# Two-layer transformer trunk: new order of the feed-forward units, later sums of one pair's rows, a second buffer for row sums

## The chip, the cores and the metric

One core of a Trainium2 chip. The metric is the device time of one execution in microseconds (us). Timed runs of the kernel before: 947.54, 944.46 and 944.89 us, median 944.89 us.

## The reference

Two decoder layers on 512 tokens of 1024 features, all in float32. Layer 0 mixes by causal pooling, layer 1 by differential attention; each mixer and each SwiGLU feed-forward is followed by a LayerNorm of the residual. The change touches the feed-forward and the LayerNorm ahead of it:

```
def _swiglu(x, w_gate, w_up, w_down):
    return (jax.nn.silu(x @ w_gate) * (x @ w_up)) @ w_down
...
for i in range(DEPTH):
    h = pool or attention
    x = _layernorm(ALPHA * x + h, ln_mix_g[i], ln_mix_b[i])
    x = _layernorm(ALPHA * x + _swiglu(x, w_gate[i], w_up[i], w_down[i]), ln_ffn_g[i], ln_ffn_b[i])
```

The hidden width is 2816, that is 22 blocks of 128 features.

## The kernel before

Float32 products are made of three products of split operands: a tile t is cast to a high part h (a cast on ACT, "CAST"), and DVE forms the low part l = t - h; PE then sums h·h, h·l and l·h. In the trace g_25h and g_25l are the two parts of weight chunk 25.

**Feed-forward, gate phase.** `hid` holds the 22 rows (blocks) of the hidden activation, transposed, in 22 rows of 512 tokens. The work is a list of units, in the order of the table `ORDER`. A plain unit f makes one hidden block: two products of 24 matmuls of width 512 (gate and up), then silu on ACT and a multiplication on DVE (`gated`, L737). A pair p(k) makes rows k and k+11 at once by a Winograd scheme of seven products in place of eight, each of 24 matmuls of width 256 (`strassen`; products in the order of `GATE`: P1, Q5, P6, Q3, P7, P2, Q4; accumulators A, B, C in PSUM). Of pairs 3 and 4 (`PRE`) the products P1 and P2 are made at the start of the phase, and their result waits in a tile `pre_g`; these are the begun pairs, of five products each (`BEGUN`: P6, Q5, P7, Q3, Q4). A pair needs four raw weight rows of 128x1024 from the wall of weights in HBM, three of its seven chunks are sums of rows (L696, DVE), every chunk is split (cast L699 on ACT, low part L702 on DVE). The products of a pair take as left operands blocks of x (`xt`) and four sums of blocks of x (`xs`), which `sums_of_x` computes step by step (L750 adds two blocks whole; L765, L767, L770, L774 the rest; casts L753, low parts L756) with four spare places in rows of `hid` as scratch (`spare`).

How far ahead chunks are made is a fixed number: after product j of a pair the steps up to chunk j + `lookahead` are issued; after a product of a plain unit, up to j + 5. Raw rows are fetched by SP into five buffers (L141), each as soon as a buffer is free; buffers of split weights are six pairs.

**Work on the side.** Generators that are stepped once after each product (`catch_up`):
- `weight_sums` / `sum_terms(k)`: sums of rows of the down-projection weights. POOL loads them (`load_terms`: two loads L804, then a third that adds in flight, L805, into rows 7 to 10 of `hid` or into the buffer of tag "gb", named b_3, b_5, ... in the trace); DVE adds twice (L810, L811); ACT stores to the DRAM tensor `tsum` (L815); then the next terms are loaded. Terms 0 and 1 are loaded at the start, 3 after unit f3 (it needs the gb buffer), each other one behind the store of the terms two before it.
- `sum_hidden(k)`: sums of the four quarters of the hidden rows k and k+11: four DVE operations of 128x256 (L836 to L839), a cast on ACT into the tile v (L841), the low part on DVE (L843), a store on ACT's queue into the DRAM tensor `ssum` (L845). v has one buffer. `SPARED` = {3: 7, 4: 10} delays pair 3's sums to product Q3 of pair 7 and pair 4's to product Q3 of pair 10.

**Down phase.** Another Winograd scheme over items d_0, d_1, ...: raw rows r_j from the wall or from `tsum`, cast to d_jh (L153, ACT), low part d_jl (L154, DVE); left operands from `hid` by a cast and a subtraction into xs, or from `ssum`; `prepare(j + 5, j + 4)` works five weight items ahead; products at L1066 into P and Q. d_5 is the last item of its first product P1, whose left operand comes from row 10 of `hid`, made by pair 10.

**LayerNorm and turning.** Four row blocks of x (128 tokens each) are normalized in turn and transposed by PE; ACT applies scale and bias into y (L280), ACT and DVE split y into `xt` (`turn`). `load_gb` loads scale and bias of the next LayerNorm into the gb buffer (L207, L208, on SP's queue); `affine` uses them on DVE (L258, L259).

Engines run their queues in program order; ACT's queue also issues the stores L815 and L845, SP's the raw rows, r rows and load_gb, POOL's the terms.

Of the kernel before, what the change touches and what calls it, by code (L numbers as in the profile page):

```python
# [18 lines left out]
P = 128  # L19
S = 512  # L20
# [28 lines left out]
SPLIT = (3, 4, 5, 6, 7, 8, 9, 10)  # L49
EARLY = (1, 0)  # L50
PRE = SPLIT[:2]
SUMS = 2
SPARED = {3: 7, 4: 10}


ORDER = "f0 f1 f2 f3 f4 p3 f5 p4 p5 p6 p7 p8 p9 p10".split()


def units(layer):
# [2 lines left out]


def lookahead(k, p):
    return 4 if k in PRE else 6 if k > 5 else 4 if p in ("P1", "Q5", "P6") else 5


AFFINE = {("P6", 2): (0, 1), ("P6", 3): (1, 1), ("Q3", 1): (2, 0), ("Q3", 2): (3, 0)}
# [6 lines left out]
def trunk(ctx, tc, x, wall, pscale, lam_p, subln, table, lng, lnb, band, first, onehot, out):  # L75
# [129 lines left out]
    def load_gb(n):  # L205
        gb = keep.tile([P, 2, D], F32, tag="gb", name=f"gb{n}")
        nc.sync.dma_start(out=gb[:, 0, :], in_=lng[n : n + 1, :].broadcast_to([P, D]))  # L207
        nc.sync.dma_start(out=gb[:, 1, :], in_=lnb[n : n + 1, :].broadcast_to([P, D]))  # L208
        gbs[n] = gb
# [107 lines left out]
        for i in (1, 0):  # L317
            nc.vector.tensor_tensor(ls[i], ys[i], hs[i].bitcast(F32), op=ALU.subtract)

    def turn(n, s):  # L320
        transposed(n, s)
        turned(n, s)

    flip, flipped = transposed, turned

# [239 lines left out]
    def ffn(layer, late):  # L565
# [7 lines left out]
        with tc.tile_pool(name=f"ffn{layer}", bufs=1) as fp:  # L573
# [168 lines left out]
            def spare(row):  # L742
                return hid[:, row : row + 2, :].rearrange("p r (a t) -> p (r a) t", a=2)

            def sums_of_x():

                r0, r1, r2, r3 = spare(3), spare(14), spare(5), spare(16)

                def whole(t, a, b):
                    tt(t, quarter(a, 0, b).bitcast(F32), quarter(a, 1, b).bitcast(F32), op=ALU.add)  # L750

                def high(m, t):
                    nc.scalar.copy(xs[:, m, 0], t)  # L753

                def low(m, t):
                    tt(xs[:, m, 1], t, xs[:, m, 0].bitcast(F32), op=ALU.subtract)  # L756

                whole(r2, 0, 0)
                yield
                whole(r3, 0, 1)  # L760
                yield
                whole(r0, 1, 0)
                whole(r1, 1, 1)
                yield
                tt(r1, r0, r1, op=ALU.subtract)  # L765
                high(0, r1)
                tt(r0, r2, r0, op=ALU.subtract)  # L767
                high(2, r0)
                yield
                tt(r2, r1, r2, op=ALU.subtract)  # L770
                high(1, r2)
                low(0, r1)
                yield
                tt(r3, r3, r2, op=ALU.add)  # L774
                high(3, r3)
                low(1, r2)
                yield
                low(2, r0)
                yield
                low(3, r3)  # L780
                yield
# [48 lines left out]
            def sum_hidden(k):  # L830

                first, second = hid[:, k, :256], hid[:, k, 256:]
                a12, a22 = hid[:, k + HALF, :256], hid[:, k + HALF, 256:]
                u = fp.tile([P, 2, 256], F32, tag="u", name=f"u{layer}_{k}", bufs=1)
                v = fp.tile([P, 2, 2, 256], F32R, tag="v", name=f"v{layer}_{k}", bufs=1)
                tt(u[:, 0, :], first, second, op=ALU.subtract)  # L836
                tt(second, second, a22, op=ALU.subtract)
                tt(u[:, 1, :], a12, first, op=ALU.subtract)
                tt(u[:, 1, :], u[:, 1, :], second, op=ALU.add)  # L839
                yield  # L840
                nc.scalar.copy(v[:, :, 0, :], u)  # L841
                yield
                tt(v[:, :, 1, :], u, v[:, :, 0, :].bitcast(F32), op=ALU.subtract)  # L843
                yield
                nc.scalar.dma_start(out=ssum[:, :, :, k, :], in_=v.bitcast(F32))  # L845
# [77 lines left out]
            by_half = [(0, 0, ks[0]), (1, 0, ks[0]), (0, 0, ks[1]), (1, 0, ks[1])]  # L923
            by_half += [(0, 1, ks[1]), (0, 1, ks[0])]
            halved = [(w, e, ks[b]) for b in range(2) for w, e in ((0, 0), (1, 0), (0, 1))]
            pre_g = {k: fp.tile([P, S], F32, name=f"g{layer}_{k}") for k in PRE}
            pre_a = {}
            products = [0]

            def turn_late():  # L930
                products[0] += 1
                if products[0] in late:
                    late[products[0]]()

            ready_first = 2 * early + 2 * len(PRE) + (early == 0)
            for lo in (0, 256):
# [34 lines left out]
            def plain(f):  # L971
                k = f // 2
                j = number[f, 0]
                a = (bank(f"g{layer}_{f}"), bank(f"u{layer}_{f}"))
                for i in range(2):
                    product(a[i], j + i, 0, S, by_part if f == i == 0 else None)
                    if f >= SUMS:
                        next(sums, None)
                    ahead(j + i + 5)
                    catch_up()  # L980
                gated(order[f], *a)
                if f < SB:
                    affine(n - 1, f, f // 2)
                if f % 2 or f == 0:
                    weight_sums()
                if f == 3:
                    load_terms(3)
                if f % 2 and k not in SPARED:
                    behind.append(sum_hidden(k))

            def strassen(k):
# [10 lines left out]
                for p in BEGUN if begun else GATE:  # L1002
# [30 lines left out]
                    elif p == "Q4":  # L1033
                        tt(first, both(g0), first, op=ALU.mult)
                        tt(second, both(g1), second, op=ALU.mult)
                if k < HALF - 1:
                    weight_sums()
                if k not in SPARED:
                    behind.append(sum_hidden(k))

            for kind, i in units(layer):
                (plain if kind == "f" else strassen)(i)
            load_gb(n - 1)
            while behind:
                catch_up()
            fetched[0] = divided[0] = c1 + FB
# [29 lines left out]
            for p in DOWN:  # L1076
# [7 lines left out]
                for i in range(together):  # L1084
                    j = j0 + i
                    prepare(j + 5, j + 4)
                    if p == "Q4":
                        if i == together - 1:
                            prepare(len(items), len(items))
                            ready(c1 + FB + 2)  # L1090
                        for s in range(2):
                            if i == s:
                                spread_of(n, s)
                            if i == s + 1:
                                norm(n, s)
                    if (p, i) == ("Q4", 2) and not final:
                        tall_step(2)
                    multiply(j, accs, range(2))
                    if (p, i) in AFFINE:
                        affine(n - 1, *AFFINE[p, i])  # L1100
                        if final and (p, i) == list(AFFINE)[-1]:
                            load_gb(n)
# [41 lines left out]
    def attention():  # L1144
        n = 2
        with tc.tile_pool(name="attn", bufs=1) as ap:
# [406 lines left out]
            for s in range(SB):  # L1553
                acc = gather(1, s, ws)
                if s == 0:
                    ready(where[0] + 1)
                for d in range(2):
                    residual(s, d, acc[d], 1.0)
                    stat(n, s, d)
                spread_of(n, s)  # L1560
                if s > 0:
                    turn(n, s - 1)
                norm(n, s)
                ready(where[0] + (min(s + 1, WBUFS - 4) if s < 3 else 4))
            base[0] = where[0]

    def later(n, s):
        return lambda: turn(n, s)

    ffn(0, {3: later(0, 2), 5: later(0, 3)})  # L1570
    attention()
    ffn(1, {2: later(2, 3)})


def buckets(rel):
# [105 lines left out]
```

## Time and profile before

| | |
|---|---|
| profiled execution | 949.09 us |
| its span | 947.3 us (1.8 us of the execution lie around it) |
| median of the timed runs | 944.89 us (944.46 to 947.54) |
| PE, DVE, ACT, POOL busy | 926.9, 803.5, 518.7, 127.3 us |
| HBM traffic | 217.39 MB, mean 229 GB/s |
| the first down product begins, layer 0 and layer 1 | about 265 us, about 829 us |

A row of a timeline gives start and duration of an instruction, its engine, line and tiles, and in brackets how long its engine stood idle before it and what ended that. Matmuls overlap: their starts are 0.227 us apart at width 512 and 0.120 us at width 256, while each is listed as 0.39 and 0.28 us long, so a stop of PE is read from starts, as the distance of two starts less that pitch.

### The profile page before, as it was taken

How to read it: one execution, taken by the hardware profiler on the slowest of the kernel's cores; microseconds unless marked ns; L12 is line 12 of the kernel's file. 1: busy time of each engine (PE TensorE's matmuls, PEld its weight loads, DVE VectorE, ACT ScalarE, POOL GpSimd, SP SyncE). 2: the span in 40 equal slices, each digit the busy share in tenths (PEclk: the TensorE clock that was granted, in tenths of full speed). 3: DMA queues.
4: the chain of work that ended last, by engine and by line, in shares of the span. 5: the costliest groups of instructions: out<-in, count | busy, mean ns of one | idle time of the engine just before them, and what ended most of it. 6: DMA issues, size and time to landing. Idle time of an engine off the chain costs nothing.

```text
span 947.3 us, 14914 instructions
## 1 busy us (share of the span) xinstructions
PE 926.9 (98%) x5662; PEld 824.0 (87%) x5662; DVE 803.5 (85%) x1190; ACT 518.7 (55%) x826; POOL 127.3 (13%) x152
## 2 busy tenths in 40 slices
PE   9999999999989999999999999999999999989996
PEld 8988999999978888888888888988999999968885
DVE  7988789999878897868888877868799999768888
ACT  6663335554545467767878754824444545554460
POOL 4111211110001201201112000210111110001101
PEclk9999999999999999999999999999999999999999
DMA  8496989986777988965666522693988985778962
GB/s 236 157 291 217 291 281 298 274 268 233 235 229 273 348 292 236 223 199 153 163 135 184 151 67 68 195 322 104 310 282 280 310 263 195 244 229 271 372 212 89
DMA packets 87765, 217.39 MB, mean 229 GB/s; under 512 B 15332, under 2 KB 26852, under 8 KB 87694
## 3 DMA queue, kind: packets, MB, share of 16 engines
q1 hardware_dynamic: 45148, 123.46, 38.1%
q0 software_dynamic: 18768, 58.20, 25.2%
q10 hardware_dynamic: 23778, 34.78, 10.1%
q8 instruction: 44, 0.72, 0.3%
q14 instruction: 27, 0.22, 0.1%
HBM read 179.70 MB, written 36.72 MB: 228 GB/s over the span
## 4 chain that ended last, share of the span: by engine, by line
PE 57%; DVE 23%; DMA 8%; issue 6%; ACT 4%; POOL 1%; ACTq 1%; DVEq 0%; POOLq 0%; SPq 0%
PE P L1066 10%; PE Q L1066 6%; PE A L906 6%; DVE raw L696 4%; PE C L906 3%; DMA raw<-in_wall 3%; DMA b<-in_wall 3%; PE va L1220 2%; PE B L906 2%; PE s L1289 2%; PE q L179 2%; PE q L181 2%; PE k L179 2%; PE k L181 2%; PE q L180 2%
## 5 line engine op out<-in xcount | busy, mean ns | idle before, releaser
L696 DVE TENSOR_TENSOR raw<-raw,raw 128x1024 f32<-128x1024 f32 x64 | 78.2, 1222 | 8.9 <-DMA raw<-in_wall 8.0
L153 ACT CAST xs<-hid 128x512 fp32r<-128x512 f32 (+1 forms) x60 | 34.7, 581 | 26.8 <-DVE hid L873 26.8
L154 DVE TENSOR_TENSOR xs<-hid,xs 128x512 fp32r<-128x512 f32 (+1 forms) x60 | 38.4, 642 | 7.8 <-ACT xs L153 7.8
L1309 ACT ACTIVATE p<-p,mn 128x128 f32<-128x128 f32 (+3 forms) x64 | 35.2, 552 | 14.1 <-DVE mn L1304 14.1
L841 ACT CAST v<-u 128x512 fp32r<-128x512 f32 x22 | 13.7, 621 | 52.3 <-DVE u L839 34.9
L280 ACT ACTIVATE y<-pt,bT,gT 128x128 f32<-128x128 f32 x72 | 27.1, 456 | 23.5 <-PE pt L266 18.0
L804 POOL DMA_DIRECT2D b<-in_wall x20 | 14.1, 708 | 189.3 <-DMA tsum<-b 58.3
L865 POOL DMA_DIRECT2D xs<-ssum x24 | 17.5, 727 | 148.9 <-PE Q L1066 73.0
L229 POOL TENSOR_TENSOR rs<-rs,mhalf 128x1 f32<-128x1 f32 x16 | 12.9, 806 | 138.3 <-DVE rs L228 93.6
L1304 DVE CUSTOM_DVE_ANT_0 p<-s,bias 128x128 f32<-128x128 f32 (+3 forms) x64 | 28.0, 485 | 1.1 <-PE s L1289 1.1
L1012 ACT COPY hid<-C 128x512 f32<-128x512 f32 x16 | 9.4, 588 | 35.1 <-PE A L906 12.2
L804 POOL DMA_DIRECT2D hid<-in_wall x24 | 20.9, 913 | 56.0 <-DMA tsum<-hid 28.8
L753 ACT CAST xs<-hid 128x1024 fp32r<-128x1024 f32 x8 | 8.4, 1050 | 28.5 <-DVE hid L765 15.6
L220 DVE BATCH_NORM_STATS2 st<-res 128x6 f32<-128x512 f32 x32 | 22.2, 695 | 1.1
L843 DVE TENSOR_TENSOR v<-u,v 128x512 fp32r<-128x512 f32 x22 | 15.1, 686 | 9.0 <-ACT v L841 9.0
L805 POOL DMA_DIRECT2D hid<-in_wall x12 | 14.8, 1233 | 55.2 <-DMA hid<-in_wall 55.2
L737 DVE TENSOR_TENSOR hid<-sg,u 128x512 f32<-128x512 f32 x12 | 8.2, 686 | 13.5 <-PE u L181 7.3
L154 DVE TENSOR_TENSOR xt<-y,xt 128x512 fp32r<-128x512 f32 x18 | 12.2, 689 | 8.7 <-ACT xt L153 8.7
L1323 DVE SCALAR_TENSOR_TENSOR p<-p,sm,p 128x128 f32<-128x128 f32 (+3 forms) x32 | 17.6, 551 | 1.1
L805 POOL DMA_DIRECT2D b<-in_wall x10 | 12.3, 1230 | 43.2 <-DMA b<-in_wall 43.2
L154 POOL TENSOR_TENSOR sql<-sq,sqh 128x512 fp32r<-128x512 f32 x7 | 9.3, 1324 | 60.5 <-ACT sqh L153 60.5
L259 DVE TENSOR_TENSOR res<-res,gb 128x512 f32<-128x512 f32 (+1 forms) x20 | 16.0, 799 | 0.7
(1206 smaller groups left out, 3583.3 us busy)
## 6 DMA issues: line engine op xcount, KB each, us to landing
raw<-in_wall SPq DMA_DIRECT2D x130, 512.0 KB, 5.7
r<-tsum SPq DMA_DIRECT2D x40, 512.0 KB, 4.3
hid<-in_wall POOLq DMA_DIRECT2D x36, 512.0 KB, 8.0
b<-in_wall POOLq DMA_DIRECT2D x30, 512.0 KB, 6.3
r<-in_wall SPq DMA_DIRECT2D x30, 512.0 KB, 5.6
tsum<-hid ACTq DMA_DIRECT2D x24, 512.0 KB, 5.8
ssum<-v ACTq DMA_DIRECT2D x22, 512.0 KB, 5.5
tsum<-b ACTq DMA_DIRECT2D x20, 512.0 KB, 5.7
```

The costliest lines, as they stand in the source:

```text
L153: nc.scalar.copy(dst_h, src)
L154: (low or nc.vector).tensor_tensor(dst_l, src, dst_h.bitcast(F32), op=ALU.subtract)
L179: nc.tensor.matmul(acc, ah, bh, start=start, stop=False)
L181: nc.tensor.matmul(acc, al, bh, start=False, stop=stop)
L280: nc.scalar.activation(y[:, k, :], pt[:, k * P : (k + 1) * P], AF.Identity, bias=bT[:, n, kk : kk + 1], scale=gT[:, n, kk : kk + 1],)
L696: tt(t, raws[pair[0]], raws[pair[1]], op=ALU.add)
L804: nc.gpsimd.dma_start(out=t[:, j], in_=src[:, j])
L805: nc.gpsimd.dma_start(out=t[:, 0], in_=src[:, :, 1], accum_op=ALU.add)
L906: nc.tensor.matmul(acc[:, f * 256 : (f + 1) * 256], w[:, c], x[:, kk, :], start=start and i == 0, stop=stop and i == len(todo) - 1, skip_g ...
L1066: nc.tensor.matmul(accs[s], x[:, k, r], y[:, c], start=first and k == 0 and e == 0, stop=last and k == m - 1 and e == 2, skip_group_check= ...
L1304: nc.vector.tensor_tensor_reduce(out=p, in0=accs[c], in1=biases[h][:, w - 1 :: -1] if w < S else biases[h][:, ::-1], op0=ALU.add, op1=ALU. ...
L1309: nc.scalar.activation(p, p, AF.Exp, bias=mn[:, q, c : c + 1], scale=-1.0, accum_out=sm[:, q, c : c + 1],)
```

## The change

1. `ORDER` becomes f0 f1 f2 f3 **p3 f4 p4 f5** p5 ...: a plain unit behind each begun pair (before: f3 f4 p3 f5 p4 p5). The rows of the wall follow. `lookahead` is 4 in begun pairs and 6 in all others.
2. `pre_g` of pairs 3 and 4 lies in rows 2 and 13 of `hid`, and v has two buffers.
3. `weight_sums` runs after f0 f1 f2 f4 p4 f5 p5 ... p9 (before: f0 f1 f3 p3 f5 p4 p5 ... p9): 11 times a layer as before.
4. `SPARED` = {2: 6}: the sums of hidden rows of pair 2 are made in pair 6; those of pairs 3 and 4 right behind their pairs.
5. Blocks 2 and 3 of x are turned with y written straight into the two scratch places of `sums_of_x` that held those blocks' whole sums, so two DVE additions (L750) a layer go; `sums_of_x` starts at f1 and is a step shorter. In layer 1 the turn of block 2 moves from the end of attention to the start of the feed-forward.
6. `load_gb` moves from the end of the gate phase to the second item of the down product Q5.

```diff
--- before.py
+++ after.py
@@ -49,11 +49,12 @@
 SPLIT = (3, 4, 5, 6, 7, 8, 9, 10)
 EARLY = (1, 0)
 PRE = SPLIT[:2]
-SUMS = 2
-SPARED = {3: 7, 4: 10}
-
-
-ORDER = "f0 f1 f2 f3 f4 p3 f5 p4 p5 p6 p7 p8 p9 p10".split()
+SUMS = 1
+NO_SUMS = (3, 3, 10)
+SPARED = {2: 6}
+
+
+ORDER = "f0 f1 f2 f3 p3 f4 p4 f5 p5 p6 p7 p8 p9 p10".split()
 
 
 def units(layer):
@@ -62,7 +63,7 @@
 
 
 def lookahead(k, p):
-    return 4 if k in PRE else 6 if k > 5 else 4 if p in ("P1", "Q5", "P6") else 5
+    return 4 if k in PRE else 6
 
 
 AFFINE = {("P6", 2): (0, 1), ("P6", 3): (1, 1), ("Q3", 1): (2, 0), ("Q3", 2): (3, 0)}
@@ -317,9 +318,9 @@
         for i in (1, 0):
             nc.vector.tensor_tensor(ls[i], ys[i], hs[i].bitcast(F32), op=ALU.subtract)
 
-    def turn(n, s):
+    def turn(n, s, kept=None):
         transposed(n, s)
-        turned(n, s)
+        turned(n, s, kept)
 
     flip, flipped = transposed, turned
 
@@ -742,9 +743,12 @@
             def spare(row):
                 return hid[:, row : row + 2, :].rearrange("p r (a t) -> p (r a) t", a=2)
 
+            second_half = spare(3), spare(14)
+
             def sums_of_x():
 
-                r0, r1, r2, r3 = spare(3), spare(14), spare(5), spare(16)
+                r0, r1 = second_half
+                r2, r3 = spare(5), spare(16)
 
                 def whole(t, a, b):
                     tt(t, quarter(a, 0, b).bitcast(F32), quarter(a, 1, b).bitcast(F32), op=ALU.add)
@@ -758,9 +762,6 @@
                 whole(r2, 0, 0)
                 yield
                 whole(r3, 0, 1)
-                yield
-                whole(r0, 1, 0)
-                whole(r1, 1, 1)
                 yield
                 tt(r1, r0, r1, op=ALU.subtract)
                 high(0, r1)
@@ -832,7 +833,7 @@
                 first, second = hid[:, k, :256], hid[:, k, 256:]
                 a12, a22 = hid[:, k + HALF, :256], hid[:, k + HALF, 256:]
                 u = fp.tile([P, 2, 256], F32, tag="u", name=f"u{layer}_{k}", bufs=1)
-                v = fp.tile([P, 2, 2, 256], F32R, tag="v", name=f"v{layer}_{k}", bufs=1)
+                v = fp.tile([P, 2, 2, 256], F32R, tag="v", name=f"v{layer}_{k}", bufs=2)
                 tt(u[:, 0, :], first, second, op=ALU.subtract)
                 tt(second, second, a22, op=ALU.subtract)
                 tt(u[:, 1, :], a12, first, op=ALU.subtract)
@@ -923,14 +924,16 @@
             by_half = [(0, 0, ks[0]), (1, 0, ks[0]), (0, 0, ks[1]), (1, 0, ks[1])]
             by_half += [(0, 1, ks[1]), (0, 1, ks[0])]
             halved = [(w, e, ks[b]) for b in range(2) for w, e in ((0, 0), (1, 0), (0, 1))]
-            pre_g = {k: fp.tile([P, S], F32, name=f"g{layer}_{k}") for k in PRE}
+            pre_g = {k: hid[:, r, :] for k, r in zip(PRE, (2, 2 + HALF))}
             pre_a = {}
             products = [0]
 
             def turn_late():
+                if products[0] in late:
+                    turn(n - 1, late[products[0]], second_half)
                 products[0] += 1
-                if products[0] in late:
-                    late[products[0]]()
+
+            turn_late()
 
             ready_first = 2 * early + 2 * len(PRE) + (early == 0)
             for lo in (0, 256):
@@ -981,7 +984,7 @@
                 gated(order[f], *a)
                 if f < SB:
                     affine(n - 1, f, f // 2)
-                if f % 2 or f == 0:
+                if f not in NO_SUMS:
                     weight_sums()
                 if f == 3:
                     load_terms(3)
@@ -1033,14 +1036,13 @@
                     elif p == "Q4":
                         tt(first, both(g0), first, op=ALU.mult)
                         tt(second, both(g1), second, op=ALU.mult)
-                if k < HALF - 1:
+                if k not in NO_SUMS[1:]:
                     weight_sums()
                 if k not in SPARED:
                     behind.append(sum_hidden(k))
 
             for kind, i in units(layer):
                 (plain if kind == "f" else strassen)(i)
-            load_gb(n - 1)
             while behind:
                 catch_up()
             fetched[0] = divided[0] = c1 + FB
@@ -1096,6 +1098,8 @@
                     if (p, i) == ("Q4", 2) and not final:
                         tall_step(2)
                     multiply(j, accs, range(2))
+                    if (p, i) == ("Q5", 1):
+                        load_gb(n - 1)
                     if (p, i) in AFFINE:
                         affine(n - 1, *AFFINE[p, i])
                         if final and (p, i) == list(AFFINE)[-1]:
@@ -1558,18 +1562,15 @@
                     residual(s, d, acc[d], 1.0)
                     stat(n, s, d)
                 spread_of(n, s)
-                if s > 0:
+                if 0 < s < 3:
                     turn(n, s - 1)
                 norm(n, s)
                 ready(where[0] + (min(s + 1, WBUFS - 4) if s < 3 else 4))
             base[0] = where[0]
 
-    def later(n, s):
-        return lambda: turn(n, s)
-
-    ffn(0, {3: later(0, 2), 5: later(0, 3)})
+    ffn(0, {3: 2, 5: 3})
     attention()
-    ffn(1, {2: later(2, 3)})
+    ffn(1, {0: 2, 2: 3})
 
 
 def buckets(rel):
```

The first place is ACT at the end of pair 10 and the start of the down phase of layer 0 (sg_10: the gates of pair 10; v_9, v_10, v_4: hidden sums of pairs 9, 10 and 4; xs: left operands of the down phase). Before:

```order
L841 CAST v_4_2935<-u_4_2934 128x2x256
L1032 ACTIVATE sg_10_0_2964<-B_4_683 128x512
L1026 ACTIVATE sg_10_1_2999<-A_10_2766 128x512
L153 CAST d_4h<-r_4_2858 128x1024
L153 CAST xs_538<-hid_537 128x512
L845 DMA ssum_540<-v_4_2935 512x1x256
L841 CAST v_10_3017<-u_10_3016 128x2x256
L845 DMA ssum_540<-v_10_3017 512x1x256
L153 CAST d_5h<-r_5_2892 128x512
L153 CAST d_6h<-r_6_2926 128x1024
L153 CAST xs_538<-hid_537 128x256
```

After the change:

```order
L154 CAST d_3h<-r_3_2830 128x1024
L154 CAST xs_538<-hid_537 128x512
L1035 ACTIVATE sg_10_0_2959<-B_4_679 128x512
L1029 ACTIVATE sg_10_1_2993<-A_10_2767 128x512
L154 CAST d_4h<-r_4_2859 128x1024
L154 CAST xs_538<-hid_537 128x512
L842 CAST v_10_3006<-u_10_3005 128x2x256
L846 DMA ssum_540<-v_10_3006 512x1x256
L154 CAST d_5h<-r_5_2893 128x512
L154 CAST d_6h<-r_6_2927 128x1024
L154 CAST xs_538<-hid_537 128x256
```

The pair 4 work (cast and store of v_4) is gone from here; between the gates of pair 10 and d_5h stands v_10 alone, and of the two buffers of v it takes the one that v_9 doesn't hold (v_9's store stands nine rows ahead of it).

The second place is DVE around the weight sums of terms 3 (b_3). Before, they follow pair 3 (C_3, A_3: its accumulators; sg_3_1: its second gate; g_21 to g_24: chunks of pair 4):

```order
L702 TENSOR_TENSOR g_22l<-raw_1205,g_22h 128x1024
L696 TENSOR_TENSOR raw_1205<-raw_1205,raw_1243 128x1024
L702 TENSOR_TENSOR g_21l<-raw_1205,g_21h 128x1024
L1034 TENSOR_TENSOR hid_537<-g_3_549,hid_537 128x2x256
L1035 TENSOR_TENSOR hid_537<-sg_3_1_1302,hid_537 128x2x256
L810 TENSOR_TENSOR b_3_1078<-b_3_1078 128x512
L811 TENSOR_TENSOR b_3_1078<-b_3_1078 128x512
L702 TENSOR_TENSOR g_23l<-raw_1208,g_23h 128x1024
L702 TENSOR_TENSOR g_24l<-raw_1243,g_24h 128x1024
```

After the change, they follow f4 (sg_2: the gate of hidden block 2, unit f4) and stand ahead of the chunks that pair 4's last product uses (g_23):

```order
L703 TENSOR_TENSOR g_21l<-raw_1133,g_21h 128x1024
L837 TENSOR_TENSOR u_3_1279<-hid_537 128x256
L838 TENSOR_TENSOR hid_537<-hid_537 128x256
L839 TENSOR_TENSOR u_3_1279<-hid_537 128x256
L840 TENSOR_TENSOR u_3_1279<-u_3_1279,hid_537 128x256
L703 TENSOR_TENSOR g_22l<-raw_1168,g_22h 128x1024
L738 TENSOR_TENSOR hid_537<-sg_2_1313,u_4_1253 128x512
L811 TENSOR_TENSOR b_3_1069<-b_3_1069 128x512
L812 TENSOR_TENSOR b_3_1069<-b_3_1069 128x512
L844 TENSOR_TENSOR v_3_1280<-u_3_1279,v_3_1280 128x2x256
L697 TENSOR_TENSOR raw_1130<-raw_1130,raw_1201 128x1024
L703 TENSOR_TENSOR g_23l<-raw_1130,g_23h 128x1024
```

The hidden sums of pair 3 (u_3, v_3) now stand here, and the weight sum stands between the low part of g_22 and the raw sum of g_23.

The third place is POOL's queue at the same time (hid: terms 0, 1, 2, 4, ... in rows of `hid`; b_3, b_5: terms 3 and 5). Before:

```order
L804 DMA hid_537<-in_wall 128x2x512 x2
L805 DMA hid_537<-in_wall 128x2x512
L804 DMA b_3_1078<-in_wall 128x2x512 x2
L805 DMA b_3_1078<-in_wall 128x2x512
L804 DMA hid_537<-in_wall 128x2x512 x2
L805 DMA hid_537<-in_wall 128x2x512
L804 DMA b_5_1356<-in_wall 128x2x512 x2
L805 DMA b_5_1356<-in_wall 128x2x512
```

After the change:

```order
L805 DMA hid_537<-in_wall 128x2x512 x2
L806 DMA hid_537<-in_wall 128x2x512
L805 DMA hid_537<-in_wall 128x2x512 x2
L806 DMA hid_537<-in_wall 128x2x512
L805 DMA b_3_1069<-in_wall 128x2x512 x2
L806 DMA b_3_1069<-in_wall 128x2x512
L805 DMA b_5_1347<-in_wall 128x2x512 x2
L806 DMA b_5_1347<-in_wall 128x2x512
```

The loads of terms 4 stand ahead of those of terms 3 now, and b_5's directly behind b_3's.

## The prediction

> **What bounds the kernel now.** First the page: who is busy (PEld: weight loads, beside PE).
>
> ```profile
> PE 926.9 (98%) x5662; PEld 824.0 (87%) x5662; DVE 803.5 (85%) x1190; ACT 518.7 (55%) x826; POOL 127.3 (13%) x152
> ```
>
> PE is the bound, and the change adds and removes no matmul; all it can give or take is time in which PE stands. DVE is second, at 85% on average. Whom PE waits for is in PE's view of waits (total us, times, longest):
>
> ```profile
> PE P L1066 <- ACT xs L153: 4.3, 2, 2.3
> PE C L906 <- ACT hid L1012: 2.4, 3, 1.0
> ...
> PE P L1066 <- DVE xs L154: 1.1, 2, 0.6
> PE A L906 <- DVE hid L1021: 1.0, 3, 0.4
> PE A L906 <- DVE g_28l L702: 0.5, 2, 0.3
> PE g L719 <- ACT xt L153: 0.3, 1, 0.3
> PE A L906 <- ACT g L1018: 0.2, 1, 0.2
> ```
>
> Two places, then: the first down products (P, L1066, once a layer), and pairs of the gate phase (A and C, L906). Windows of 25 us around both show more (PE, PEld, DVE, ACT, POOL busy, granted clock, DMA share):
>
> ```profile
> 100.00:125.00 25.00, 25.00 (x169) 23.15 (x168) 18.32 (x21) 10.24 (x13) 4.32 (x5) 1.00 0.98 301
> 125.00:150.00 25.00, 24.51 (x196) 23.86 (x195) 23.59 (x30) 9.80 (x13) 4.86 (x6) 1.00 0.89 284
> 150.00:175.00 25.00, 24.34 (x201) 23.98 (x201) 23.34 (x27) 14.06 (x18) 3.27 (x4) 1.00 0.97 292
> 175.00:200.00 25.00, 24.56 (x204) 24.36 (x204) 23.99 (x29) 12.61 (x16) 4.17 (x5) 1.00 0.94 300
> 825.00:850.00 25.00, 21.82 (x104) 17.63 (x104) 17.80 (x28) 12.25 (x20) 0.00 (x0) 0.95 0.71 230
> 850.00:875.00 25.00, 25.00 (x110) 20.64 (x109) 20.79 (x29) 12.03 (x17) 3.75 (x6) 0.98 0.80 266
> ```
>
> Around plain units (100 to 125) DVE is idle for 6.7 us of 25; as soon as pairs stand in a row (from 125) it is over 93% busy, and PE begins to lose time.
>
> **Edit 4 and v's second buffer: the first down product.** PE's timeline in layer 0, then in layer 1:
>
> ```profile
> 278.81 0.39 PE L1066 MATMUL P<-d_4h,xs 128*128 128x512 f32 x1
> 281.17 0.50 PE L1066 MATMUL P<-d_5h,xs 128*128 128x512 f32 x1 [1.98 <-ACT xs L153]
> 281.50 0.40 PE L1066 MATMUL P<-d_5l,xs 128*128 128x512 f32 x1
> 282.46 0.73 PE L1066 MATMUL P<-d_5h,xs 128*128 128x512 f32 x2 [0.56 <-DVE xs L154]
> ```
>
> ```profile
> 842.62 0.39 PE L1066 MATMUL P<-d_4h,xs 128*128 128x512 f32 x1
> 845.34 0.50 PE L1066 MATMUL P<-d_5h,xs 128*128 128x512 f32 x1 [2.34 <-ACT xs L153]
> 845.68 0.39 PE L1066 MATMUL P<-d_5l,xs 128*128 128x512 f32 x1
> 846.63 0.74 PE L1066 MATMUL P<-d_5h,xs 128*128 128x512 f32 x2 [0.56 <-DVE xs L154]
> ```
>
> Distance of starts less the pitch of 0.227: 2.13 + 0.73 = 2.86 us in layer 0, 2.49 + 0.72 = 3.21 us in layer 1. Why ACT was late is in its rows of layer 0 and of layer 1:
>
> ```profile
> 277.31 0.62 ACT L841 CAST v<-u 128x512 fp32r<-128x512 f32 x1 [8.51 <-DMA ssum<-v]
> ```
>
> ```profile
> 841.48 0.62 ACT L841 CAST v<-u 128x512 fp32r<-128x512 f32 x1 [8.88 <-DMA ssum<-v]
> ```
>
> The cast of v_10 waits for the store of v_4 to leave the only v, and d_5h and the xs cast stand behind it on ACT. Its input was there long before, by DVE's rows of each layer:
>
> ```profile
> 273.23 0.42 DVE L839 TENSOR_TENSOR u<-u,hid 128x256 f32<-128x256 f32 x1
> ```
>
> ```profile
> 837.04 0.42 DVE L839 TENSOR_TENSOR u<-u,hid 128x256 f32<-128x256 f32 x1
> ```
>
> After the change pair 4's sums are gone from here, and v has two buffers. Either alone frees v_10 from the store. Its cast can start at 273.7 in place of 277.31 (3.6 us earlier) and at 837.5 in place of 841.48 (4.0). With the rest of the chain unchanged PE's d_5 product would be ready at 277.6 and 841.3, and PE wants it at 279.04 and 842.85: late next, with 1.4 to 1.5 us to spare, is the same chain of casts, which the missing pair 4 work only shortens. **Term: -2.86 and -3.21, together -6.1 us.** In layer 1 the clock falls behind the stall: 0.95 and 0.98 in the two windows, 25 x 0.05 + 25 x 0.02 = 1.75 us lost.
>
> [...]
>
> I take the dip as removed from the profiled execution (-1.7) but not from the median, since one of two like stalls had none.
>
> **Edits 1, 3, 4: pairs 4 to 6.** PE's, DVE's, ACT's and POOL's rows around pair 5 in layer 0:
>
> ```profile
> 150.42 0.28 PE L906 MATMUL A<-xs,g_28l 128*128 128x256 f32 x1
> 151.36 0.50 PE L906 MATMUL C<-xs,g_29h 128*128 128x256 f32 x2 [0.66 <-ACT hid L1012]
> ```
>
> ```profile
> 149.59 0.69 DVE L811 TENSOR_TENSOR b<-b 128x512 f32<-128x512 f32 x1
> ```
>
> ```profile
> 98.90 1.48 POOL L804 DMA_DIRECT2D b<-in_wall  x2 [16.75 <-DVE res L259]
> ...
> 115.13 1.24 POOL L805 DMA_DIRECT2D hid<-in_wall  x1 [7.05 <-DMA hid<-in_wall]
> 131.89 1.48 POOL L804 DMA_DIRECT2D b<-in_wall  x2 [15.53 <-DVE hid L810]
> ```
>
> 0.94 - 0.12 = 0.82 us: the store of b_5 (L815) sits on ACT in front of the copy L1012, until DVE's L811 is done at 150.28, because b_5's loads began only at 131.89; the sums (L810, just ahead of this L811) had to wait for them until 148.9, 17 us later. The waits at pairs 4 to 6 in the view above are of this kind: C <- hid (2.4, of which one of 1.0 is late in layer 1 and stays), A <- L1021 (1.0, 0.4 of it at pair 6), g_28l (0.5), g (0.2). By modelled ends that is 1.4 + 0.4 + 0.5 + 0.2 = 2.5 us; from starts a wait is 0.16 us longer (0.82 against 0.66), and six of them make about 3.5. With f4 between pairs 3 and 4 and f5 ahead of pair 5, each begun pair is followed by some 10.9 us of PE (48 x 0.227) with little DVE work, instead of p4 and p5 in a row; lookahead 6 lets DVE use it. b_5 is loaded directly behind b_3, so earlier. **Term: 0 to -3.5, taken -3.0.**
>
> What they cost. DVE's work between 100 and 200 is 89.2 us of 100 (sum of four windows); pair 3's and 4's hidden sums come in (from pairs 7 and 10) with 4 x 0.42 + 0.69 = 2.4 us each, pair 2's only move within it: 94. Some 6 us stay idle, 1.5 in each window: enough if nothing lands late. With f4 behind pair 3 instead of ahead of it, pair 4 begins where f5 began before, by PE's row,
>
> ```profile
> 115.63 0.40 PE L179 MATMUL g<-xt,g_19h 128*128 128x512 f32 x1
> ```
>
> at 115.6 and not 11 us later. In DVE's rows before,
>
> ```profile
> 119.82 1.23 DVE L696 TENSOR_TENSOR raw<-raw,raw 128x1024 f32<-128x1024 f32 x1 [0.46 <-DMA raw<-in_wall]
> ...
> 124.61 1.23 DVE L702 TENSOR_TENSOR g_21l<-raw,g_21h 128x1024 fp32r<-128x1024 f32 x1 [1.17 <-ACT g_21h L699]
> ```
>
> ```profile
> raw<-in_wall SPq DMA_DIRECT2D x130, 512.0 KB, 5.7
> ```
>
> its first low part is done 6.0 us after its third raw row is there. Pair 3 now starts 25.3 us ahead of 115.6 (14.4 for its own 120 matmuls of 0.120, 10.9 for f4), at 90.3. The third row's buffer is freed by pair 3's last low part, wanted at 90.3 + 4 x 2.88 = 101.8, and put by me at 102.4; with 5.7 us, the median, it lands at 108, with 10 (DMA is 0.98 busy here) at 112.4, so the low part is done at 114 to 118.4 against a need at 115.9: a stall of 0 to 2.5 us, nearer 0.8; in layer 1, with the same order, 0 to 1, nearer 0.3. Pair 3's own last chunk has 0 to 0.4. **Term: +0 to +4, taken +1.5.**
>
> **Edits 5 and 6.** In the view by lines:
>
> ```profile
> L750 DVE TENSOR_TENSOR hid<-xt 128x1024 f32<-128x1024 f32 x8 | 9.6, 1218 | 0.0
> ```
>
> Four of eight go, 4.9 us of DVE, all beside PE's work on f0 to f3 and the first products of pairs 3 and 4, so at 0; without that cover it would be a gain of up to 4.9. y in `hid` and layer 1's turn keep PE's order, at 0, or -0.3 (the wait of g for xt). load_gb moves behind r_15 on SP, and is used seven items after, some 17 us later at 2.7 us each (12 x 0.227): 0; were it later, DVE would wait in `affine` with weights of Q3 behind it. Moving it off r_9's way helps SP, not PE: 0.
>
> **Sum.** -6.1 - 3.0 + 1.5 = -7.6, and -1.7 for the dip, brings the profiled 949.09 to about 939.8. The median, 4.2 us lower, gets -7.6: **937.3 us**.
>
> **Rivals.**
> (a) The begun pairs pay: both upper ends of 0 to 4, DVE at 94% over the stretch, and half of the pairs' gain: -6.1 - 1.5 + 4 = -3.6, 941.3 us. For it: DMA share 0.98 at 100 to 125; against: each f behind a pair gives DVE 5 us.
> (b) Slower: b_3. Its loads now wait behind terms 4's on POOL. Terms 4 wait for the store of terms 2, whose sum now follows f2 (f2 ends one unit before 90.3, at 79.4; sum to about 84, stored to about 93); their two loads and the load that adds are issued over some 9 to 10 us (7.05 of it a wait at 115.13, before), then b_3's from about 103, done 17 us later like b_5's: 120. DVE is in order, and behind L811 of b_3 stand the sum and split of the chunk of pair 4's last product, wanted at 115.6 + 4 x 2.88 = 127.2; they take 1.3 + 0.6 + 2.4 us, so b_3 must land by 122.9. Each us beyond costs PE one, in both layers. Landing at 129 or later (6 us each, 12 together) gives -7.6 + 12: 949 us. It turns slower from 127 on. Against it: that is 7 us more than b_5's load took.
> (c) Down stall only replaced: ACT still late at d_5 (the casts of pair 10's gates and d_4h stand ahead, 1.4 us to spare): half of 6.1 back, 940.3 us; if both v's release and pair 4's absence did nothing, 943.4.
> (d) The dip too belongs to the median: 935.6 us.
>
> **Chances.** Forecast with (d) 0.62, (a) 0.16, (c) 0.10, (b) 0.12 (with smaller late loads inside it). 0.3% is 2.8 us, about what a measurement of this kernel can tell from no change: bounds 942.1 and 947.7. Faster 0.80 (forecast, most of (a) and (c)), same 0.10, slower 0.10. Range 932.0 to 944.0: the low end is the forecast with no cost (-1.5), the dip gone (-1.7) and 2 us of pair waits beyond my 3; the high end takes in (a) and (c) and leaves out (b).
>
> **What would show it.** Right: no row of ACT L842 released by a DMA; no wait of P for xs in the view of waits, clock 1.00 around 850; waits of A and C below 2 us. (a): stops of PE at the start of pair 4 (g_19l); (b): DVE L811 on b_3 released by a DMA after 123; (c): P <- ACT xs stays, behind another releaser. The prediction is wrong if PE's new stops at pairs 3 and 4 exceed 7 us together.

## The result, and the profile after

934.37 us median of 6 runs (933.01 to 935.4) against 944.68 of 6 runs of the kernel before (941.84 to 947.54): ratio 0.9889, 95% interval 0.9869 to 0.9909, 10.3 us less. The prediction said 937.3, with 932.0 to 944.0 as its range. The profiled execution has a span of 933.6 us, 13.7 less than the one before. PE's view of waits after the change:

```profile
PE A L907 <- DVE hid L1024: 3.1, 3, 1.4
PE warm L387 <- POOL ident masks.py:199: 1.9, 1, 1.9
PE va L1224 <- DVE vals L1414: 0.2, 1, 0.2
PE pool L436 <- ACT fh L154: 0.2, 1, 0.2
PE pt L267 <- DVE res L239: 0.2, 1, 0.2
```

No row of P (the down products) is left, none of C, and one of A. That one is 3.1 us long in all, so one of the signs that the prediction gave for being right, waits of A and C below 2 us, did not come true; the others did. The windows that answer to those shown of before:

```profile
100.00:125.00 25.00, 24.25 (x159) 22.18 (x159) 19.89 (x25) 10.82 (x15) 1.37 (x2) 1.00 0.97 279
125.00:150.00 25.00, 25.00 (x168) 23.11 (x167) 23.56 (x29) 13.15 (x17) 5.40 (x6) 1.00 0.91 286
150.00:175.00 25.00, 24.00 (x201) 23.80 (x200) 21.15 (x25) 10.50 (x13) 3.46 (x4) 1.00 1.00 307
175.00:200.00 25.00, 25.00 (x210) 24.88 (x209) 24.72 (x32) 13.56 (x17) 3.43 (x4) 1.00 0.84 260
825.00:850.00 25.00, 25.00 (x112) 20.71 (x111) 20.81 (x30) 14.96 (x21) 0.34 (x1) 1.00 0.71 231
850.00:875.00 25.00, 25.00 (x112) 20.71 (x111) 22.07 (x30) 10.80 (x14) 7.67 (x11) 1.00 0.97 358
```

The clock is 1.00 around 850, and PE is full where it lost 3 us to the stop at d_5 in layer 1. ACT's rows of the second v at the end of pair 10, in layer 0 and layer 1, name no DMA now:

```profile
269.30 0.62 ACT L842 CAST v<-u 128x512 fp32r<-128x512 f32 x1 [4.30 <-DVE u L840]
```

```profile
827.16 0.62 ACT L842 CAST v<-u 128x512 fp32r<-128x512 f32 x1 [4.30 <-DVE u L840]
```

PE goes from d_4 to d_5 at its pitch, 0.22 us from start to start:

```profile
276.15 0.39 PE L1068 MATMUL P<-d_4h,xs 128*128 128x512 f32 x1
276.37 0.39 PE L1068 MATMUL P<-d_5h,xs 128*128 128x512 f32 x1
```

What is left in the gate phases are three stops before a pair's last product Q4, which overwrites accumulator A: 0.9 us at pair 3 and 1.2 at pair 5 in layer 0, 1.5 at pair 5 in layer 1. DVE's rows at pair 5 of layer 0:

```profile
155.78 1.23 DVE L697 TENSOR_TENSOR raw<-raw,raw 128x1024 f32<-128x1024 f32 x1 [1.81 <-DMA raw<-in_wall]
156.93 1.22 DVE L703 TENSOR_TENSOR g_34l<-raw,g_34h 128x1024 fp32r<-128x1024 f32 x1
158.06 0.68 DVE L1024 TENSOR_TENSOR hid<-hid,A 128x512 f32<-128x512 f32 x1
```

DVE waited 1.81 us for a raw row of pair 6, a sum made ahead; L1024, which frees A, stood two rows behind it, and PE stood until 158.80.

Balance of the two traces, in starts less pitch, stops over 0.25 us: gone are 6.1 at d_5 and 0.3 at d_6 behind it, 3.75 at pairs 4 to 6, 2.1 at pair 10 and 0.4 at the start of the gate phase, and 1.7 of the clock dip; come are 3.6 at pairs 3 and 5. That is 10.7 of 13.7; the other 3.0 are what is left, in the main stops under 0.25 us each. The median's gain is 10.3: the profiled execution of before lies 4.4 us above its median, that of after 1.0 above its own, so the profiled gain isn't the one to compare with.

### The profile page after: what moved, and what is told of

The parts are those of the page before. It is cut to its first block, busy times and chain, and to the rows that moved or that the text cites. A ratio compares the mean times of both kernels' runs of the same rounds, so it can differ in the third digit from the quotient of the medians.

```text
span 933.6 us, 14893 instructions
## 1 busy us (share of the span) xinstructions
PE 919.7 (99%) x5662; PEld 821.5 (88%) x5662; DVE 799.7 (86%) x1186; ACT 521.0 (56%) x826; POOL 127.0 (14%) x152
## 4 chain that ended last, share of the span: by engine, by line
PE 77%; DVE 12%; DMA 4%; ACT 3%; issue 2%; ACTq 0%; DVEq 0%; POOL 0%; SPq 0%
PE A L907 16%; PE P L1068 14%; PE C L907 7%; PE Q L1068 6%; PE B L907 4%; DMA raw<-in_wall 3%; DVE raw L697 2%; PE s L1293 2%; PE va L1224 2%; PE q L180 1%; PE q L182 1%; PE k L180 1%; PE k L182 1%; PE q L181 1%; PE k L181 1%
## 5 line engine op out<-in xcount | busy, mean ns | idle before, releaser
L697 DVE TENSOR_TENSOR raw<-raw,raw 128x1024 f32<-128x1024 f32 x64 | 78.2, 1222 | 10.3 <-DMA raw<-in_wall 9.4
L842 ACT CAST v<-u 128x512 fp32r<-128x512 f32 x22 | 13.7, 621 | 43.5 <-DVE u L840 43.5
L281 ACT ACTIVATE y<-pt,bT,gT 128x128 f32<-128x128 f32 x40 | 15.1, 456 | 15.8 <-PE pt L267 15.8
L1029 ACT ACTIVATE sg<-A 128x512 f32<-128x512 f32 x16 | 9.6, 598 | 21.7 <-PE A L907 21.7
L1022 DVE TENSOR_TENSOR hid<-C,hid 128x512 f32<-128x512 f32 x16 | 11.0, 689 | 9.3 <-PE C L907 6.8
```

The lines of the kernel that those rows point to most:

```text
L697: tt(t, raws[pair[0]], raws[pair[1]], op=ALU.add)
```

## The experiments

**Which part freed d_5.** First each of its two parts undone in the changed kernel, one buffer for v:

```diff
-                v = fp.tile([P, 2, 2, 256], F32R, tag="v", name=f"v{layer}_{k}", bufs=2)
+                v = fp.tile([P, 2, 2, 256], F32R, tag="v", name=f"v{layer}_{k}", bufs=1)
```

> The changed kernel with one buffer for v instead of two, all else as changed. My theory: the stall at d_5 went because pair 4's sums left the end of pair 10, and the second buffer only doubles that; v_9's store is issued nine rows ahead of v_10's cast, so nothing waits: no stall of PE at d_5, time as the changed kernel (about 934, within 1.5 us). Rival (the second buffer is what removed it): the stalls of 2.1 to 2.5 and 0.7 us at d_5 are back in both layers, about 940.

Measured 935.6 us, ratio to the kernel before 0.9897 (0.9854 to 0.9939); no stop at d_5. The second buffer alone isn't what did it. Then pair 4's sums put back into pair 10:

```diff
-SPARED = {2: 6}
+SPARED = {2: 6, 4: 10}
```

> The changed kernel with pair 4's hidden sums back in pair 10 (SPARED 2:6 and 4:10), v with two buffers. My theory: v_10's cast takes the other buffer than v_4's, but v_9's store must be gone: it is, so no wait on a store; PE has no stall at d_5 or one under 0.7 us, since ACT and DVE have 2.4 us more work right ahead of it; DVE has 2.4 us less around pair 5. Time 933 to 936. Rival (the end of pair 10 is too full in itself): stalls of 2 us and more at d_5 in both layers, 938 to 940.

Measured 933.51 us, ratio 0.9867 (0.9832 to 0.9901); no stop at d_5, and none at pair 5 either in its trace. So far both as I held: in neither run does v_10's cast wait for a store. Both undone at once, with the two edits above:

> The changed kernel with both undone: pair 4's hidden sums in pair 10 and one buffer for v. My theory: the cast of v_10 waits some 8 us for the store of v_4, PE stalls 2.9 and 3.2 us at d_5 as before: 6 us more than the changed kernel, about 940.5. Rival: the stalls do not come back, about 934.5, and the gain was made elsewhere.

Measured 934.58 us, ratio 0.9881 (0.9842 to 0.992). My expectation fell: no stop at d_5. The wait itself is back; ACT's rows of this run at the end of pair 10, v_4's store and v_10's cast:

```profile
265.92 0.52 ACTq L846 DMA_DIRECT2D ssum<-v  x1
270.13 0.62 ACT L842 CAST v<-u 128x512 fp32r<-128x512 f32 x1 [6.25 <-DMA ssum<-v]
```

But store to cast took 4.2 us (3.7 in layer 1), while the rows of before are

```profile
270.82 0.54 ACTq L845 DMA_DIRECT2D ssum<-v  x1
277.31 0.62 ACT L841 CAST v<-u 128x512 fp32r<-128x512 f32 x1 [8.51 <-DMA ssum<-v]
```

6.5 us (6.8 in layer 1). What made the store slow then? SP's queue before has two transfers of 512 KB just ahead of it, load_gb, which edit 6 moves:

```profile
267.49 0.33 SPq L207 DMA_DIRECT2D gb<-in_lng  x1
267.87 0.42 SPq L208 DMA_DIRECT2D gb<-in_lnb  x1
```

So all three undone:

```diff
-SPARED = {2: 6}
+SPARED = {2: 6, 4: 10}
...
+            load_gb(n - 1)
             while behind:
                 catch_up()
...
-                    if (p, i) == ("Q5", 1):
-                        load_gb(n - 1)
```

> The changed kernel with pair 4's hidden sums in pair 10, one buffer for v, and load_gb back at the end of the gate phase. In the run without the last of these v_10 still waited 6 us for v_4's store, but PE did not stop, since the store took 3.7 to 4.2 us and not 6.5 to 6.8. New theory: the store is slow where the two transfers of load_gb are issued 3 us ahead of it; then it takes 6 us or more here, and PE stops at d_5 by 1 to 2.5 us in each layer: 936 to 939. Rival (the store is faster since everything at the end of pair 10 is about 1 us earlier against PE): the store takes about 4 us again, no stop, 934.5.

Measured 938.29 us, ratio 0.9933 (0.9912 to 0.9954). The store is slow again, 6.1 us by ACT's rows (5.5 in layer 1),

```profile
270.05 0.52 ACTq L846 DMA_DIRECT2D ssum<-v  x1
276.19 0.62 ACT L842 CAST v<-u 128x512 fp32r<-128x512 f32 x1 [8.18 <-DMA ssum<-v]
```

and PE stops again at d_5:

```profile
279.16 0.39 PE L1069 MATMUL P<-d_4h,xs 128*128 128x512 f32 x1
280.08 0.50 PE L1069 MATMUL P<-d_5h,xs 128*128 128x512 f32 x1 [0.53 <-ACT xs L154]
280.42 0.40 PE L1069 MATMUL P<-d_5l,xs 128*128 128x512 f32 x1
281.37 0.73 PE L1069 MATMUL P<-d_5h,xs 128*128 128x512 f32 x2 [0.56 <-DVE xs L155]
```

0.69 + 0.73 us here, 0.72 in layer 1: 2.1 of the 6.1 of before, and in layer 1 less than the 1 us that I had as the least. In the changed kernel, then, the stop came back in the run with three things at once: one v, pair 4's sums in pair 10, and load_gb in front of the store. That moving load_gb suffices is shown by the run with two undone, and that moving pair 4's sums suffices by the next run; that a second v alone would suffice, with the other two as before, was not run. The other 4 us of the 6.1 go with two differences that the rows show: the store is issued 4.3 us behind the first down product here and 5.4 before, and it takes 0.4 to 1.3 us less. (In the run with the order alone, below, it is issued 4.3 and 5.4 us behind in the two layers, takes 6.5 and 6.7 us, and PE stops for 2.1 and 3.1 us.) Which part of the change moved the store was not tried. This run has more stops that are no part of it (0.8 and 1.5 at pair 3, 0.7 and 0.5 at pair 4), so it is in part luck that its time fits the forecast.

The same part alone, in the kernel before:

```diff
-SPARED = {3: 7, 4: 10}
+SPARED = {3: 7}
```

> The kernel before with one part of the change alone: pair 4's hidden sums right behind pair 4 (SPARED 3:7 only), one v, the old order of units. My theory: both stalls at d_5 go (-6.1 us), but DVE, over 93% busy from pair 4 on, gets 2.4 us more work at pair 5, where PE already waits for it: +1 to +4 us over both layers; in all 939 to 943. Rival (the room made by the new order is not needed): the whole 6 us, 938.5 or less.

Measured 941.04 us, ratio 0.9944 (0.9918 to 0.997), 5.3 us less than before, inside what the theory gave. No stop at d_5, and none at pair 10. Those at pairs 5 and 6 are in its view of waits, now with C and A waiting on ACT at pair 5; together they are 4.8 us, against 3.75 at pairs 4 to 6 before:

```profile
PE C L906 <- ACT hid L1012: 1.3, 2, 0.7
PE A L906 <- ACT hid L1014: 1.3, 2, 0.7
PE A L906 <- DVE hid L1021: 0.8, 2, 0.4
PE A L906 <- DVE g_28l L702: 0.3, 1, 0.3
```

**The order of units.** Alone, in the kernel before (sums of x a unit earlier, since pair 3 needs them):

```diff
-ORDER = "f0 f1 f2 f3 f4 p3 f5 p4 p5 p6 p7 p8 p9 p10".split()
+ORDER = "f0 f1 f2 f3 p3 f4 p4 f5 p5 p6 p7 p8 p9 p10".split()
...
-SUMS = 2
+SUMS = 1
```

> The kernel before with the order of units alone (f3 p3 f4 p4 f5 p5, sums of x from f1 on; lookahead, SPARED, v, pre_g, load_gb and the whole sums as before). Theory: the stops at pairs 4 to 6 go (about -3.5 us over both layers), those at d_5 stay (-0): 941 to 943. Rival: all engines run ahead through the whole gate phase, so the d_5 chain too comes out in time: 936 to 938.

Measured 946.84 us, ratio 1.0017 (0.9995 to 1.0039): nothing gained, against both expectations. Its view of waits shows where it went:

```profile
PE P L1066 <- ACT xs L153: 3.4, 2, 2.2
PE A L906 <- DVE hid L1021: 3.1, 3, 1.6
...
PE C L906 <- ACT hid L1012: 1.6, 1, 1.6
```

The stops at pairs 4 and 5 are gone, 0.3 of those at pair 6 is left, and pair 3 has new ones: 1.72 before Q3 and 1.75 before Q4 in layer 0, 1.38 in layer 1. Those at d_5 stayed (5.2 of 6.1 us), with the store at 6.5 and 6.7 us behind load_gb. The order alone moves the shortage on DVE from pairs 4 to 6 to pair 3; it doesn't remove it.

The other way round, the old order in the changed kernel, with pre_g in tiles of its own and one v:

> The changed kernel with the old order of units (f3 f4 p3 f5 p4 p5); pre_g therefore in tiles of its own and v with one buffer, all else as changed. Theory: PE's stops at pairs 4 to 6 are back (0.4, 0.4, 0.8 and 0.6 us in layer 0, 0.3, 0.4 and 0.8 in layer 1, some more since the hidden sums of pairs 3 and 4 now stand there), those at the last products of pairs 3 and 5 go, none at d_5: 935 to 938. Rival (the order is worth nothing in itself): 933 to 934.5, at or under the changed kernel.

Measured 967.66 us, ratio 1.02 (1.0145 to 1.0255), outside both expectations. The weight sums stood at the wrong unit for it: those of terms 3 follow f4, which now ended ahead of pair 3. DVE's row on b_3, and ACT's behind it:

```profile
119.83 0.69 DVE L811 TENSOR_TENSOR b<-b 128x512 f32<-128x512 f32 x1 [14.92 <-DMA b<-in_wall]
```

```profile
119.75 1.89 ACTq L816 DMA_DIRECT2D tsum<-b  x2
121.68 0.58 ACT L1015 COPY hid<-C 128x512 f32<-128x512 f32 x1 [17.02 <-DVE b L812]
```

PE stood 13.8 us in layer 0 and 10.2 in layer 1 for that copy. This is the mechanism of rival (b), with its price; what the order is worth in the changed kernel this run can't tell, and the old order with the weight sums at their old units too was not run.

**What makes room ahead of pair 3.** Edit 5's turn undone (y in tiles, the whole sums of blocks 2 and 3 by DVE):

```diff
-                    turn(n - 1, late[products[0]], second_half)
+                    turn(n - 1, late[products[0]])
...
                 whole(r3, 0, 1)
                 yield
+                whole(r0, 1, 0)
+                whole(r1, 1, 1)
+                yield
```

> The changed kernel with edit 5's turn undone: blocks 2 and 3 turned through y tiles, their whole sums formed by the two additions of 128x1024 in a step of their own. The prediction costs them at nothing, hidden behind PE on f0 to f3: 934 to 935. Theory now: they are 2.4 us more of DVE ahead of pair 3, where DVE is the one that PE waits for: stops at pair 3 of 2 to 3.3 us in layer 0 and 0 to 1.5 in layer 1, 936 to 938.

Measured 940.58 us, ratio 0.9932 (0.9901 to 0.9963), 4.1 us above the changed kernel by the ratios (0.0043 x 944.7), though the two intervals overlap a little; against the changed kernel's second run below (0.9899) it is 3.1. The trace agrees in size: stops of 0.40, 1.18 and 2.29 at the start and pair 3 of layer 0 and 1.16 in layer 1, 5.0 in place of 0.9. PE's rows at pair 3 (in this run's numbering L1027 is the subtraction that frees A):

```profile
96.74 0.51 PE L910 MATMUL A<-xs,g_14h 128*128 128x256 f32 x2 [1.02 <-ACT hid L1020]
...
104.89 0.47 PE L910 MATMUL A<-xt,g_16h 128*128 128x256 f32 x2 [2.13 <-DVE hid L1027]
```

So the theory put forward for this run held in its mechanism, and the prediction's price of nothing did not. The time is above the theory's 936 to 938: the stops at pair 3 of layer 0, 3.5 us, were a little longer than it had, and the clock fell behind them (0.93 in the window of 100 to 125, last section), which it didn't count. The run undoes the additions, their step and the way through the y tiles together; which of them costs what was not taken apart. The weight sums at their old units instead:

```diff
-                if f not in NO_SUMS:
+                if f % 2 or f == 0:
...
-                if k not in NO_SUMS[1:]:
+                if k < HALF - 1:
```

> The changed kernel with the weight sums at their old units (f0 f1 f3 p3 p4 f5 p5 to p9), all else as changed. Theory (what the order needs is room on DVE ahead of pair 3, since the order alone only moved PE's stops to pair 3): the two additions, 1.4 us, now stand behind f3 instead of f2, ahead of pair 3's last chunks, and those of terms 3 behind pair 3: the stop at pair 3's last product grows from 0.9 to about 2 us in layer 0 and appears with up to 1 us in layer 1; 1 to 3 us more than the changed kernel, 936 to 938. Rival (the place of these sums does not matter, and b_3's later load behind terms 4 was the only risk in it): 934 to 935.

Measured 936.35 us, ratio 0.9876 (0.9822 to 0.993). My theory fell: pair 3's stop is 0.94 us in layer 0, none in layer 1, as in the changed kernel. In the new order the place of these sums makes no difference that its trace shows; the timed runs alone could not tell less than some 5 us.

**Two attempts at more.** The changed kernel was run once more beside the first:

> The changed kernel itself once more, as the measure for the runs beside it: 934, PE's stops of 0.9 us at pair 3's last product again (A waited for from DVE L1024), those of 1.2 and 1.5 us at pair 5's last product only where a raw row lands late on DVE.

Measured 935.31 us, ratio 0.9899 (0.9874 to 0.9923); stops 0.93 at pair 3, 0.48 at pair 4, 2.23 and 0.65 at pair 5. The first attempt:

```diff
 def lookahead(k, p):
+    if (k, p) == (3, "Q5"):
+        return 3
+    if (k, p) == (5, "Q3"):
+        return 5
     return 4 if k in PRE else 6
```

> The changed kernel with lookahead 3 behind product Q5 of pair 3 and 5 behind Q3 of pair 5, which on DVE only moves the two subtractions L1024 that free the accumulator A ahead of the raw sums and the splits made ahead. Theory: PE's stops at the last products of pairs 3 and 5 (0.9, 1.2 and 1.5 us in the changed kernel's trace) come from a raw sum that stands ahead of L1024 in DVE's queue; they go, 1 to 3.5 us less than the changed kernel: 931 to 933. Rival (what is moved back is then late for pair 6 or for pair 3's last chunk): the stops appear one product later, 934 or more.

Measured 939.08 us, ratio 0.9939 (0.9916 to 0.9961): the rival was right. L1024 (L1028 here) comes in time now, but the raw sum behind it is late for its own chunk, as PE's rows of this run show:

```profile
101.93 0.50 PE L911 MATMUL A<-xt,g_16h 128*128 128x256 f32 x2 [0.19 <-ACT g_16h L704]
103.19 0.39 PE L911 MATMUL A<-xt,g_16l 128*128 128x256 f32 x1 [0.76 <-DVE g_16l L707]
```

It is 0.35 + 0.92 us in place of 0.93 at pair 3 of layer 0, and 1.27 in layer 1, where there was nothing; 0.92 at the first low part of pair 4 in layer 0; about 0.4 each at pairs 6 and 7 in both layers. The stops at pair 5 (2.23 and 0.65 us in the run beside it) are gone, against 1.5 us in all at pairs 6 and 7, so by the places of the stops it is the move at pair 3 that cost most; the move at pair 5 alone was not run. At pair 3 another order of DVE's rows only moved the stop; what lacks there, as I take it, is DVE time. The second attempt takes work away from there:

```diff
-SPARED = {2: 6}
+SPARED = {1: 8, 2: 6, 4: 10}
```

> A version meant to beat the changed kernel: hidden sums of pair 1 moved to pair 8 and those of pair 4 to pair 10, pair 2's at pair 6 as changed. Theory: 2.4 us less of DVE ahead of pair 3's last chunks take away the stop of 0.9 us there, and 2.4 us less behind pair 4 those at pair 5 (0.5 to 2.2): 931.5 to 933. Rival (DVE, busy for 92 to 95% from 200 to 260, has no room at pair 8): stops at pairs 8 to 10, 934 or more.

Measured 937.05 us (933.19 to 941.24), ratio 0.9893 (0.9843 to 0.9943). In its trace the stops at pairs 3 and 5 are gone, with 0.34 and 0.45 us at pair 10 instead, and its span is 931.4 us; the timed runs spread too wide to call it better. The same holds for 933.51 us of the version with pair 4 late. No version was shown to beat the changed kernel.

## Why the prediction was right, and where it was not

- **The first down product: right, -6.1 forecast, 6.1 found.** The cast of v_10 no longer waits for the store, and PE no longer for d_5. "Either alone frees v_10" holds for its wait, and each undone alone cost nothing that could be measured. Moving load_gb "helps SP, not PE: 0" had the mechanism wrong: in the two runs that differ in it alone, its two transfers made the store last 5.5 and 6.1 us in place of 3.7 and 4.2. It didn't show in the sum, since the other two edits remove the same stop.
- **The clock dip** went with the stop (1.00 in both windows of after, 0.95 and 0.98 in those of before), as the prediction had it for the profiled execution. Of the two like stops of before, layer 0's 2.13 + 0.73 us left the clock at 1.00 in the window of 275 to 300. Whether the dip belongs to the median, rival (d), stays open: the mean clock was 0.996 or lower in 24 of the 53 timed runs of the kernel before that stood beside the experiments, and 0.997 or 0.998 in all twelve of the changed kernel.
- **Pairs 4 to 6: the size was near (-3.0 forecast, 3.75 found), the reason was half of it.** I gave it to the new order and lookahead. The order alone does take these stops away, but 4.9 us come at pair 3 in their place, and it gains nothing. Lookahead 6 and the sums of pair 2 in pair 6 were not tried alone.
- **The step that failed is the one on edit 5**, "4.9 us of DVE, all beside PE's work ..., so at 0". This was reckoned on the old order, in which f4 stands between these additions and pair 3. With pair 3 directly behind f3 that cover is gone: with the additions back, PE stops 4.6 us at pair 3 in the two layers in place of 0.9, and the time is 3 to 4 us longer. So the edit isn't worth 0; it pays for the new order. (That the old order covers the additions was not run.)
- **The cost of the begun pairs, +1.5 forecast, 3.6 found in the trace**, 0.9 at pair 3 and the rest not where I looked for it: pair 4's first low part, feared up to 2.5 us late, was done at 114.4, 0.9 us before PE used it, while PE stopped at pair 5 in both layers, where DVE had waited for a raw row that landed late. Over the traces of the changed kernel and its variants that stop was 0 to 2.2 us in a layer.
- **Pair 10: put down as staying, but gone.** The prediction left the wait for the copy L1012 late in layer 1 where it was; that stop (1.2 us, behind the store of a weight sum) and two of A, 2.1 us in all, went too. They are also gone in the kernel before with pair 4's sums moved, so there that part alone removes them; in the changed kernel with these sums put back they did not return, so something else does it there too.
- **The size: in part luck.** By the traces the costs came out 2.1 us above the +1.5, and the 2.1 us at pair 10 make up for it by chance. The rest of what the trace gained beyond the forecast is mostly the 3.0 us of small stops. How the median's 10.3 divides can't be read from two traces.
- **Rival (b) didn't come, but it is real.** b_3's loads were issued from 98.1 and its sum ran without a wait:

```profile
120.14 0.69 DVE L811 TENSOR_TENSOR b<-b 128x512 f32<-128x512 f32 x1
```

That is 2.8 us ahead of the 122.9 that the prediction gave as the latest; the run with the old order shows what is lost when the sum comes before its load.

## What to carry to other kernels

A stop behind a wait for a store has two sizes in it: who waits (a buffer, the place of the work) and how long the store takes (here 5.5 and 6.1 us with load_gb's two transfers issued in front of it, 3.7 and 4.2 without); undo parts together as well as singly, since each alone may look worthless. Work that is hidden is hidden beside the units that run before its result is needed: when units are reordered, price again what stood behind the unit that moved. When a wait disappears after a reordering, look for the same engine's shortage at the next place before crediting the order.

## What the runs showed of the hardware

In these traces the granted clock fell after some stops of PE of 2.1 to 3.2 us in all and not after others. It fell after stops of 2.49 + 0.72 us (kernel before, layer 1: 0.95 and 0.98 in the windows of 825 to 875), of 1.33 + 0.73 and 2.38 + 0.72 (the order alone, layers 0 and 1: 0.93 in the windows of 275 to 300 and of 825 to 850), and after 2.29 us in the run with the whole sums:

```profile
100.00:125.00 25.00, 22.87 (x136) 20.81 (x135) 19.55 (x25) 10.38 (x13) 2.61 (x3) 0.93 0.83 251
```

0.07 x 25 = 1.75 us lost, three quarters of the stop itself. It stayed at 1.00 after 2.13 + 0.73 (before, layer 0, window of 275 to 300) and after 2.23 us (the changed kernel's second run, window of 150 to 175).

Narrow windows show how long it stayed down. In the run with the order alone the granted clock (the third number from the right) is at half for 3.41 us in each layer:

```profile
281.11:282.11 1.00, 0.44 (x2) 0.29 (x2) 1.00 (x3) 1.00 (x3) 0.00 (x0) 1.00 0.91 307
282.11:285.52 3.41, 3.41 (x9) 2.68 (x9) 3.41 (x5) 3.41 (x5) 0.00 (x0) 0.50 0.80 223
285.52:286.52 1.00, 1.00 (x6) 0.77 (x5) 1.00 (x2) 1.00 (x3) 0.00 (x0) 1.00 0.98 242
845.31:848.72 3.41, 3.41 (x9) 2.62 (x9) 3.41 (x5) 3.41 (x5) 0.00 (x0) 0.50 0.83 272
```

The two falls begin 563.20 us apart, 165 times 3.413. The kernel before (847.59 and, after its last product, 943.17) and the run with the whole sums (105.25 and 934.69) have theirs 28 and 243 such steps apart. So in each of these three traces the two falls lie a whole number of steps apart. That the steps run through the whole trace as a grid was not shown; it is my estimate from these three distances. Such a grid would cut the stops: in the step of 3.41 us ahead of a fall PE stood for 1.9 to 2.6 us in the four cases above; in the two without a fall it would have stood for at most 2.0 us in one step, with 2.13 us cut into 1.95 and 0.18, and 2.23 into 2.03 and 0.20. From these six cases the standing in a step that goes with a fall begins near 2 us; this is an estimate, and a rough one, since 1.9 us had a fall and 2.03 had none.
